# Scatters without mutual waits, a modulation placed behind the routing tables, and 32-token tiles for two more expert places

## The chip, the cores and the metric

The kernel runs on one core of a Trainium2 chip. Its five engines work from queues of their own: TensorE (PE, matrix products), VectorE (DVE), ScalarE (ACT), GpSimd (POOL) and SyncE (SP), the last of which mostly starts transfers. The metric is the device time of one execution in microseconds.

## The reference

The reference computes two layers of a network on 256 tokens (x) and 256 context tokens (ctx) of width 1024, in float32. Layer 0 works on all 512 tokens, layer 1 on the 256 of x. A layer derives six modulation vectors from c by one product, runs a mixer (differential attention beside a convolution of 31 taps, both gated and merged) and then a mixture of 16 experts:

```python
probs = softmax(h @ w_router + b_router)
grouped = probs.reshape(..., N_GROUPS, EXPERTS_PER_GROUP)        # 4 groups of 4
group_sel = argmax(top_k(grouped, 2)[0].sum(-1))                 # one group per token
top_p, top_i = top_k(where(expert_ok, probs, -1.0), 2)           # two experts of that group
for e in range(16):
    y = (silu(h @ w_gate[e]) * (h @ w_up[e])) @ w_down[e]        # 1024 -> 512 -> 1024
    out = out + gates[..., e:e + 1] * y
```

Each part is followed by a residual and a layer norm, with modulation by shift, scale and gate.

## The kernel before

Products that need it are computed in float32 precision from a high and a low part (`whi`, `wlo`): `mm3` issues three matmuls for one. ScalarE writes the high part (`whi<-raw`), VectorE the low part (`wlo<-raw,whi`). The experts with few tokens use plain float32 matmuls, which the profile lists as two entries each (an order of x16 is x32 in the profile).

*Routing.* `route` (lines 914 to 1065) ranks the experts of a layer by their number of tokens and gives each rank one or more places. The last VectorE steps make the tables: `si`, `sf`, `Am`, `Bm`, then eight small matmuls (line 1012), `gidx` (line 1015; which token row stands in which slot) and `sidx` (which result row), then `idx2` and `idx4`, the same for half and quarter rows. GpSimd gathers the token rows of a place by an indirect DMA (`fetch`, line 1156) from `hdr`.

*Modulation.* `ada(l, g, tag)` (from line 366) computes one of three blocks of the modulation vectors with eight loads of `w_ada`, adds the bias (line 382, `modrow`), and for block 0 transposes the result (`tr<-cp,modrow`). Block 0 of layer 1 is computed early, beside the routing of layer 0.

*Places.* `ORDER` (line 141) lists the ranks of a layer in the order of their work. Large ranks use `expert` (128 tokens and more, split products), small ones `expert64` (lines 1277 to 1320) or `expert32` (lines 1327 to 1365). `TINY` (line 107) names the ranks that take `expert32`; `room` gives the tokens that fit (32 or 64). Each is a generator in four steps (gate, up, transposition, down), and the loop in `moe` interleaves the steps of two neighbours: gate n, up n, down n−1. The 1 MB weight halves come through a ring of slots (`raw`, `m0a`, `m0b`, `m1a`), loaded by SyncE in order (line 270), each load as soon as the products on the slot's former contents are done. The down products go to `sc` (line 1310 for 64 tokens, line 1355 for 32), are copied or scaled to `y`, and are scattered to the rows of `ydr` by an indirect DMA of GpSimd (lines 1221, 1267, 1318, 1363). Tokens beyond a place's room go to a list that `overflow` works off in a loop with a count read at run time (`nover`, line 1369), after the last place. Behind it SyncE reads `ydr` back for the sum over the two experts of a token (line 1503). In layer 0 the first two blocks of `w_in` of layer 1 are loaded ahead of that loop (`first_block`).

*Order.* A scheduler places the instructions on each engine, from their dependencies (found by the memory that they touch) and its own estimates. `follow(a, b)` (line 277) keeps a behind b. All scatters of a layer write to the same DRAM array, so each of them counts as dependent on the one before.

Of the kernel before, what the change touches and what calls it, by code (L numbers as in the profile page):

```python
# [103 lines left out]
BIG = ([(2, 2), (3, 1), (4, 1), (5, 1), (6, 1), (7, 1)], [(1, 2), (2, 2), (3, 1)])  # L104
FEW = ([0, 1] + list(range(8, 16)), [0] + list(range(4, 13)))

TINY = (list(range(12, 16)), list(range(6, 13)))
PLACES = (16, 15)


# [50 lines left out]
def dit_kernel(ctx: ExitStack, tc: tile.TileContext, A, out):  # L161
# [205 lines left out]
    def ada(l, g, tag):  # L367

        ps = bank(tag)
        bv = bias.rearrange("(j q) n -> j q n", q=32)  # L370
        src = A["b_ada"][l, g * 2048:(g + 1) * 2048].rearrange("(j n) -> j n", j=4)
        for i in range(2):
            G.dma_start(bv[:, i, :], src)
        for k in range(KC):
            raw = load_raw(A["w_ada"][l, k * 128:(k + 1) * 128, g * 2048:(g + 1) * 2048])
            for j in range(4):
                PE.matmul(ps[32 * j:32 * j + 32, :], cs[:, k, :], raw[:, j * 512:(j + 1) * 512],
                          start=k == 0, stop=k == KC - 1, tile_position=(0, 32 * j))
            if k < KC - 1:
                yield  # L380
        m = small.tile([128, 512], F32, name="modrow", bufs=1)
        V.tensor_tensor(m, ps, bias, op=OP.add)
        if g == 0:
            ps = bank("tr")
            for c in range(4):
                transposed(ps[:, c * 128:(c + 1) * 128], m[:, c * 128:(c + 1) * 128])
            pv = ps.rearrange("p (c j s) -> p c j s", c=4, j=4)
            V.tensor_copy(modT[l][:, :, 0:2, :], pv[:, :, 0:2, 0:2])
            V.tensor_scalar(modT[l][:, :, 2:4, :], pv[:, :, 2:4, 0:2], 1.0, None, op0=OP.add)
        else:  # L390
            dst = moddr[l][:, g * 2048:(g + 1) * 2048].rearrange("s (j n) -> s j n", j=4)
            mv = m.rearrange("(j q) n -> j q n", q=32)
            for i in range(2):
                G.dma_start(dst[i], mv[:, i, :])
        yield
# [518 lines left out]
    def route(l, lg, first):  # L914
# [148 lines left out]
        pool_cm.close()  # L1063
        return erow, sidx, gidx, (idx2, idx4), didx, (cnt, rank, ef)

    def overflow_list(l, pool, cnt, rank, ef, sidx):

        def new(shape, name, dt=F32):
            return pool.tile(shape, dt, name=name)

        def tt_(o, a, b, op):
            V.tensor_tensor(o, a, b, op=op)

        eqc = pool.tile([128, 256], F32, name="v64", bufs=2)[0:1].rearrange("p (a b) -> p a b", a=NE)
        tt_(eqc, rank[0:1, None, :].to_broadcast([1, NE, NE]), C("iota16")[0:1, :, None].to_broadcast([1, NE, NE]),
            OP.is_equal)
        tt_(eqc, eqc, cnt[0:1, None, :].to_broadcast([1, NE, NE]), OP.mult)
        cr = new([1, NE], "cr")
        V.tensor_reduce(cr, eqc, axis=AX.X, op=OP.add)
        no = sum(t[1] for t in OVER[l])  # L1080
        act = new([1, 2, no], "oact")
        eo = new([1, no], "eo", I32)
        so = new([128, no], "so", I32)
        at = 0
        for rk, n, c, least in OVER[l]:
            to, of_ = slice(at, at + n), slice(CAP[l] * rk + c, CAP[l] * (rk + n - 1) + c + 1, CAP[l])
            V.tensor_scalar(act[:, 0, to], cr[:, rk:rk + n], float(least), None, op0=OP.is_gt)
            G.tensor_copy(eo[:, to], ef[:, rk:rk + n])
            G.tensor_copy(so[:, to], sidx[:, of_])
            at += n  # L1090
        tt_(act[:, 1, :], act[:, 0, :], C("iota")[0:1, 1:no + 1], OP.mult)
        nf = new([1, 1], "nf")
        V.tensor_reduce(nf, act[:, 1, :], axis=AX.X, op=OP.max)
        ni = cst.tile([1, 1], I32, name=f"nover{l}")
        V.tensor_copy(ni, nf)
        so_d = dram.tile([128, no], I32, name=f"so_d{l}")
        eo_d = dram.tile([1, no], I32, name=f"eo_d{l}")
        G.dma_start(so_d, so)
        G.dma_start(eo_d, eo)
        return ni, so_d, eo_d  # L1100
# [33 lines left out]
    def moe(l, lg, mh, ml, xn, early, pre_cm, pre):  # L1134
# [64 lines left out]
        def dense(raws, w, xs):  # L1199

            vs, pairs = [], [xs[i:i + 2] for i in range(0, len(xs), 2)]
            for x2 in pairs:
                for ps in up(w, x2, {6: hold["place"]} if x2 is pairs[0] else {}):
                    t = pc.tile([128, DE], F32, name="act", bufs=3)
                    S.activation(t, ps, AF.Tanh, scale=0.5)
                    V.scalar_tensor_tensor(t, t, 1.0, ps, op0=OP.add, op1=OP.mult)
                    vs.append(t)
            hold["split"], hold["logits"] = hold["oh"], None
            w = chunks(raws, 512, ((V, G), (G, V)))
            hold["split"] = None  # L1210
            pu = []
            for i, x2 in enumerate(pairs):
                for v, ps in zip(vs[2 * i:], up(w, x2, {} if i else {1: hold["index"]})):
                    V.scalar_tensor_tensor(v, v, 0.5, ps, op0=OP.mult, op1=OP.mult)
            hold["split"] = hold["gidx"]
            w = chunks(raws, D)
            hold["split"] = None
            ats = [activated(v, True) for v in vs]
            for i, py in enumerate(down(w, ats, "mm")):
                y = outrows(py)  # L1220
                G.indirect_dma_start(out=ydr[l][:, :],
                                     out_offset=bass.IndirectOffsetOnAxis(ap=didx[:, i:i + 1], axis=0),
                                     in_=y, in_offset=None, bounds_check=2 * T - 1, oob_is_err=False)

        def activated(v, rows=False):
            ps = bank("tr")
# [18 lines left out]
        def expert(raws, xs, cols):  # L1245
# [18 lines left out]
            w = chunks(raws, D)  # L1264
            for a, col in zip(ats, cols):
                y = outrows(down(w, [a], "sc")[0])
                G.indirect_dma_start(out=ydr[l][:, :],
                                     out_offset=bass.IndirectOffsetOnAxis(ap=sidx[:, col:col + 1], axis=0),
                                     in_=y, in_offset=None, bounds_check=2 * T - 1, oob_is_err=False)

        def expert64(raws, x, i, whole):

# [42 lines left out]
                V.tensor_tensor(y, py, g2h, op=OP.mult)  # L1315
            else:
                S.copy(y, py)
            G.indirect_dma_start(out=ydr[l].rearrange("t (h d) -> (t h) d", h=2),
                                 out_offset=bass.IndirectOffsetOnAxis(ap=idx2[:, 1, i:i + 1], axis=0),
                                 in_=y, in_offset=None, bounds_check=4 * T - 1, oob_is_err=False)  # L1320

        def expert32(raws, x, i):

# [36 lines left out]
                V.tensor_tensor(y, py[:, :256], g2q, op=OP.mult)  # L1360
            else:
                S.copy(y, py[:, :256])
            G.indirect_dma_start(out=ydr[l].rearrange("t (q d) -> (t q) d", q=4),
                                 out_offset=bass.IndirectOffsetOnAxis(ap=idx4[:, i:i + 1], axis=0),
                                 in_=y, in_offset=None, bounds_check=8 * T - 1, oob_is_err=False)

        def overflow(over, pc):
            ni, so_d, eo_d = over
# [294 lines left out]
```

## Time and profile before

| | us |
|---|---|
| median of 3 runs | 1284.88 (1283.53 to 1286.5) |
| the profiled execution | 1286.37 |
| its span | 1284.4 |
| TensorE busy | 1130.4 (88%) |
| VectorE busy | 748.5 (58%) |
| ScalarE busy | 453.5 (35%) |
| GpSimd busy | 217.9 (17%) |
| mean granted clock | 0.942 |

The span runs from the first to the last instruction of the profiled execution. Layer 0's routing tables end near 458 us, its experts run from 462 to about 730, the layer 1 mixer and routing follow, the small places of layer 1 begin near 1058, its last scatter leaves at 1260, and the rest is the sum over the experts with a layer norm. A row of a timeline is a group of like instructions one after another: start, time from its first start to its last end, engine, line, operation, output and inputs, shape, count; in brackets the idle time of the engine before it and what ended it. "SPq" is SyncE's queue of issued transfers; there the time is that of issuing, with what an issue waited for.

### The profile page before, as it was taken

The numbers are of one execution on the slowest core, as the hardware profiler recorded it, in microseconds if no ns is written. First come the engines' busy times: TensorE is split into PE (matmuls) and PEld (weight loads), VectorE is DVE, ScalarE is ACT, GpSimd is POOL, SyncE is SP. The second block draws the span as 40 slices with busy tenths as digits, with TensorE's granted clock in tenths as the row PEclk, the third lists the DMA queues.
The fourth block names the chain that finished last, engine by engine and source line by source line (L and its number), as shares of the span: only waits on it lengthen the run. The fifth ranks groups of instructions, "written<-read, shape, count | busy, mean of one in ns | idle before, by whom it ended". The sixth has DMA issues, their size and how long they took to land. (4 is left out here: it accounts for less than half of the span.)

```text
span 1284.4 us, 18914 instructions
## 1 busy us (share of the span) xinstructions
PE 1130.4 (88%) x7254; PEld 816.0 (64%) x7254; DVE 748.5 (58%) x1303; ACT 453.5 (35%) x767; POOL 217.9 (17%) x297
## 2 busy tenths in 40 slices
PE   4799999999999869998898558999999799997981
PEld 2476767676878445766666246666888575775751
DVE  0628987766376614355555279996658842424355
ACT  1422223445331504344454233233554621323230
POOL 2500010000000293120100121101100472110111
PEclk9799999997999979999999778999999989998986
DMA  8666651020247979898999698566327579999993
GB/s 307 205 203 224 235 196 66 33 68 32 70 168 287 399 288 394 342 418 344 387 406 417 248 326 296 198 229 225 105 100 284 219 263 372 377 418 426 408 378 110
DMA packets 81452, 336.29 MB, mean 262 GB/s; under 512 B 10398, under 2 KB 10702, under 8 KB 53456
## 3 DMA queue, kind: packets, MB, share of 16 engines
q1 hardware_dynamic: 67072, 303.06, 61.6%
q0 software_dynamic: 10656, 21.11, 4.8%
q10 hardware_dynamic: 3632, 10.90, 2.2%
q8 instruction: 58, 0.95, 0.3%
q14 instruction: 34, 0.28, 0.1%
HBM read 326.16 MB, written 17.57 MB: 268 GB/s over the span
## 5 line engine op out<-in xcount | busy, mean ns | idle before, releaser
L287 DVE TENSOR_TENSOR wlo<-raw,whi 128x1024 fp32r<-128x1024 f32 x196 | 237.9, 1233 | 107.3 <-ACT whi L286 106.2
L286 ACT CAST whi<-raw 128x1024 fp32r<-128x1024 f32 x204 | 209.8, 1049 | 220.2 <-PE mm L321 109.8
L719 DVE SCALAR_TENSOR_TENSOR cv<-cv,cwt,cv 128x512 f32<-128x512 f32 (+1 forms) x240 | 135.4, 611 | 0.7
L317 PE MATMUL mm<-hh,whi 128*128 128x512 f32 (+1 forms) x384 | 131.8, 351 | 2.1 <-ACT hh L513 1.6
L320 PE MATMUL mm<-hl,whi 128*128 128x512 f32 (+1 forms) x384 | 130.1, 343 | 2.7 <-DVE hl L517 2.6
L321 PE MATMUL mm<-hh,wlo 128*128 128x512 f32 (+1 forms) x384 | 129.1, 344 | 0.0
L317 PEld LDWEIGHTS mm<-hh,whi 128*128 128x128 f32 x384 | 73.2, 193 | 21.7 <-issue 8.1
L320 PEld LDWEIGHTS mm<-hl,whi 128*128 128x128 f32 x384 | 73.5, 192 | 16.7 <-issue 6.1
L321 PEld LDWEIGHTS mm<-hh,wlo 128*128 128x128 f32 x384 | 72.8, 192 | 14.9 <-issue 7.2
L320 PE MATMUL mm<-wlo,xt 128*128 128x512 f32 x192 | 78.1, 408 | 0.4
L317 PE MATMUL mm<-whi,xt 128*128 128x512 f32 x192 | 75.8, 403 | 1.7 <-ACT whi L286 1.7
L321 PE MATMUL mm<-whi,xt 128*128 128x512 f32 x192 | 76.8, 401 | 0.0
L320 PE MATMUL mm<-wlo,hh 128*128 128x512 f32 x176 | 70.4, 400 | 1.4 <-DVE wlo L287 1.4
L317 PE MATMUL mm<-whi,hh 128*128 128x512 f32 x176 | 69.7, 403 | 0.0
L321 PE MATMUL mm<-whi,hl 128*128 128x512 f32 x176 | 69.5, 396 | 0.0
L320 PEld LDWEIGHTS mm<-wlo,xt 128*128 128x128 f32 x192 | 37.0, 193 | 13.7 <-DVE wlo L287 4.0
L1289 PE MATMUL mm<-raw,xt 128*64 128x256 f32 x384 | 45.2, 382 | 0.0
L320 PE MATMUL sc<-wlo,at 128*128 128x512 f32 x96 | 41.1, 428 | 3.3 <-DVE wlo L287 3.1
L317 PEld LDWEIGHTS mm<-whi,xt 128*128 128x128 f32 x192 | 36.8, 193 | 10.9 <-ACT whi L286 2.6
L317 PEld LDWEIGHTS mm<-whi,hh 128*128 128x128 f32 x176 | 33.4, 190 | 15.8 <-issue 5.9
L321 PEld LDWEIGHTS mm<-whi,xt 128*128 128x128 f32 x192 | 37.0, 193 | 7.1
L668 DVE TENSOR_REDUCE mx<-sc 128x1 f32<-128x512 f32 (+1 forms) x48 | 28.4, 599 | 22.1 <-PE sc L663 21.9
(407 smaller groups left out, 2175.8 us busy)
## 6 DMA issues: line engine op xcount, KB each, us to landing
raw<-in_w_ada_dram SPq DMA_DIRECT2D x48, 1024.0 KB
raw<-in_w_e_down_dram SPq DMA_DIRECT2D x47, 1024.0 KB
raw<-in_w_e_up_dram SPq DMA_DIRECT2D x44, 1024.0 KB
raw<-in_w_e_gate_dram SPq DMA_DIRECT2D x41, 1024.0 KB
raw<-in_w_in_dram SPq DMA_DIRECT2D x36, 1024.0 KB
m0a<-in_w_e_up_dram SPq DMA_DIRECT2D x10, 1024.0 KB
raw<-in_w_out_dram SPq DMA_DIRECT2D x8, 1024.0 KB
m0b<-in_w_e_gate_dram SPq DMA_DIRECT2D x8, 1024.0 KB
```

The lines of the kernel that those rows point to most:

```text
L286: j = S.copy(hi, src)
L287: i = eng.tensor_tensor(lo, src, hi.bitcast(F32), op=OP.subtract)
L317: i = PE.matmul(ps, lhs[0], rhs[0], start=first, stop=False)
L320: PE.matmul(ps, lhs[0], rhs[1], start=False, stop=False)
L321: PE.matmul(ps, lhs[1], rhs[0], start=False, stop=last)
L668: V.tensor_reduce(mx[:, m:m + 1], pS[:, :n], axis=AX.X, op=OP.max, negate=True)
L719: i = V.scalar_tensor_tensor(av, win, cwt[:, cb, j:j + 1], av, op0=OP.mult, op1=OP.add)
L1289: PE.matmul(ps[64 * j:64 * j + 64, u * 256:u * 256 + 256], xt[:, k, k0 // 4, :], raw[:, k * 512 + j * 256:k * 512 + j * 256 + 256], start= ...
```

## The change

The scatters of a layer are declared independent of one another, by a helper that replaces the four direct calls of `dense`, `expert`, `expert64` and `expert32`. The reason given is that no two places hold the same row. The scatter inside the overflow loop stays as it was. The add of `modrow` for block 0 of layer 1 has to come behind the table `idx2`. `TINY[1]` starts at rank 4 rather than rank 6, so that places 4 and 5 of layer 1 (ranks by number of tokens) use `expert32`, gather 64 half rows rather than 128, and have room for 32 tokens; the overflow list of layer 1 is made from three entries rather than four.

```diff
-TINY = (list(range(12, 16)), list(range(6, 13)))
+TINY = (list(range(12, 16)), list(range(4, 13)))
...
         m = small.tile([128, 512], F32, name="modrow", bufs=1)
-        V.tensor_tensor(m, ps, bias, op=OP.add)
+        i = V.tensor_tensor(m, ps, bias, op=OP.add)
+        if l and g == 0:
+            follow(i, hold["route"])
...
+    def scatter(l, view, **kw):
+
+        i = G.indirect_dma_start(out=view, in_offset=None, oob_is_err=False, **kw)
+        for other in scattered[l]:
+            tc.declare_no_dep(i.ins, other.ins, reason="no two slots hold the same row")
+        scattered[l].append(i)
+
+    scattered = ([], [])
...
-            G.indirect_dma_start(out=ydr[l].rearrange("t (h d) -> (t h) d", h=2),
-                                 out_offset=bass.IndirectOffsetOnAxis(ap=idx2[:, 1, i:i + 1], axis=0),
-                                 in_=y, in_offset=None, bounds_check=4 * T - 1, oob_is_err=False)
+            scatter(l, ydr[l].rearrange("t (h d) -> (t h) d", h=2),
+                    out_offset=bass.IndirectOffsetOnAxis(ap=idx2[:, 1, i:i + 1], axis=0), in_=y, bounds_check=4 * T - 1)
```

The three other sites are replaced in the same way. Since the dependencies differ, the scheduler draws up another order. Three places follow. Line numbers of the new kernel are up to 9 higher. SyncE loads the weights in practically the same order as before.

The first is VectorE at the routing tables of layer 0. Before:

```order
L1002 TENSOR_SCALAR si<-si 128x8
L382 TENSOR_TENSOR modrow<-mm,bias 128x512
L1004 CAST sf<-si 128x16
L1007 TENSOR_TENSOR Am<-cp,sf 128x512
L1011 TENSOR_SCALAR Bm<-cp,sf 128x128 x4
L388 COPY modT_104<-tr 128x4x4
L389 TENSOR_SCALAR modT_104<-tr 128x4x4
L1011 TENSOR_SCALAR Bm<-cp,sf 128x128 x3
L1622 TENSOR_TENSOR gt_5826<-modT_104,pt_598 128x8
L1011 TENSOR_SCALAR Bm<-cp,sf 128x128
L1623 TENSOR_TENSOR bt_5827<-modT_104,pt_598 128x8
L1622 TENSOR_TENSOR gt_5826<-modT_104,pt_598 128x8
```

Now:

```order
L1004 TENSOR_SCALAR si<-si 128x8
L1006 CAST sf<-si 128x16
L1009 TENSOR_TENSOR Am<-cp,sf 128x512
L1013 TENSOR_SCALAR Bm<-cp,sf 128x128 x8
L1017 TENSOR_SCALAR gidx<-sc 128x64
L1019 TENSOR_SCALAR sidx<-sc 128x64
L1023 TENSOR_TENSOR cmp<-rank,cp 1x256
L930 TENSOR_TENSOR cmp<-cmp,cp 1x256
L1029 TENSOR_REDUCE ef<-cmp 1x16
L1031 CAST erow<-ef 1x16
L1055 TENSOR_SCALAR idx_3323<-four,cp 128x4
L1053 TENSOR_SCALAR idx_3321<-both,cp 128x20
```

Before, `modrow` stood between `si` and `sf`, and its transposed copies (`modT`, `gt`, `bt`) between the pieces of `Bm`; `gidx` came three rows below the last one shown. Now the tables come first, and `modrow` follows directly behind the last row shown.

The second is TensorE at the end of layer 0's experts. `sc<-raw_5562` and `sc<-raw_5568` are the down products of the last place but one (rank 11, 64 tokens), `xt_5517` are the tokens of the last place (rank 15), `v_5615` its hidden values, and `nover` the count of the overflow loop. Before:

```order
L321 MATMUL sc<-whi,at 128x512
L1335 MATMUL mm<-raw,xt_5517 32x128 x16
L1335 MATMUL mm<-m0a,xt_5517 32x128 x16
L324 MATMUL tr<-cp,v_5615 128x128
L1310 MATMUL sc<-raw_5562,at_5559 64x512 x4
L1310 MATMUL sc<-raw_5568,at_5559 64x512 x4
L1355 MATMUL sc<-raw,at_5621 32x256 x16
L1369 TENSOR_LOAD nover_5704
```

Now:

```order
L1343 MATMUL mm<-raw_5520,xt_5517 32x128 x9
L1343 MATMUL mm<-raw_5538,xt_5517 32x128 x16
L1319 MATMUL sc<-raw_5562,at_5559 64x512 x4
L1319 MATMUL sc<-raw_5568,at_5559 64x512 x4
L1343 MATMUL mm<-raw,xt_5517 32x128 x16
L1343 MATMUL mm<-m0a,xt_5517 32x128 x16
L324 MATMUL tr<-cp,v_5615 128x128
L1363 MATMUL sc<-raw,at_5621 32x256 x16
L1376 TENSOR_LOAD nover_5704
```

The down products of rank 11 have moved from behind the transposition of the last place to ahead of its up products. At five more places of layer 0 the down products of a place moved in the same way, ahead of the end of the next place's up products.

The third is TensorE at the end of layer 1's experts, where `sc<-whi` and `sc<-wlo` are the split down products of rank 3, `mm<-raw_10628` (now `raw_10706`) the last up products of the last place, and `sc<-raw_10655` and `sc<-m0a` (now `raw_10733`) its down products. Before:

```order
L321 MATMUL sc<-whi,at 128x512
L317 MATMUL sc<-whi,at 128x512
L320 MATMUL sc<-wlo,at 128x512
L321 MATMUL sc<-whi,at 128x512
L1335 MATMUL mm<-raw_10628,xt_10511 32x128 x16
L324 MATMUL tr<-cp,v_10646 128x128
L1355 MATMUL sc<-raw_10655,at_10652 32x256 x8
L1355 MATMUL sc<-m0a,at_10652 32x256 x8
L1369 TENSOR_LOAD nover_10712
```

Now:

```order
L321 MATMUL sc<-whi,at 128x512
L317 MATMUL sc<-whi,at 128x512 x2
L1343 MATMUL mm<-raw_10688,xt_10589 32x128 x7
L320 MATMUL sc<-wlo,at 128x512
L321 MATMUL sc<-whi,at 128x512
L320 MATMUL sc<-wlo,at 128x512
L321 MATMUL sc<-whi,at 128x512
L1343 MATMUL mm<-raw_10688,xt_10589 32x128 x9
L1343 MATMUL mm<-raw_10706,xt_10589 32x128 x16
L324 MATMUL tr<-cp,v_10724 128x128
L1363 MATMUL sc<-raw_10733,at_10730 32x256 x8
L1363 MATMUL sc<-m0a,at_10730 32x256 x8
```

Before, all split products of rank 3 stood ahead of the last up products; now a part of these stands between the split products. The down products of the place before the last (`sc<-m0a,at_10423`, now `at_10501`) were scattered in pieces of one to eight among the up products of rank 3; now they stand in two blocks of eight.

## Rows read from the trace of the kernel before

**Rows 1.** Timeline of VectorE, 445 to 450: start us, us, engine, line, operation [idle <-releaser].

```profile
445.84 0.69 DVE L382 TENSOR_TENSOR modrow<-mm,bias 128x512 f32<-128x512 f32 x1 [2.66 <-PE mm L377]
...
449.96 0.23 DVE L1015 TENSOR_SCALAR gidx<-sc 128x64 int32<-128x64 f32 x1
```

**Rows 2.** Timeline of TensorE, 444 to 458.

```profile
444.71 1.07 PE L377 MATMUL mm<-raw,cs 128*32 128x512 f32 x8 [0.33 <-DMA raw<-in_w_ada_dram]
...
447.66 0.97 PE L1012 MATMUL sc<-Am,Bm 128*128 128x64 f16 x4 [0.41 <-DVE Bm L1011]
...
457.67 1.19 PE L324 MATMUL tr<-cp,xg 64*128 64x64 f32 x8 [7.74 <-DMA xg<-hdr,gidx]
```

**Rows 3.** Timeline of GpSimd, first gather.

```profile
451.04 1.02 POOL L1156 DMA_INDIRECT xg<-hdr,gidx  x1 [3.01 <-DVE bt L1624]
```

**Rows 4.** Waits of TensorE, 480 to 715: total us, times, longest us.

```profile
PE tr L324 <- DVE v L1297: 3.8, 3, 1.5
PE tr L324 <- DVE act L1260: 3.1, 4, 0.8
```

**Rows 5.** Timeline of TensorE, end of layer 0's experts.

```profile
713.28 1.12 PE L1335 MATMUL mm<-raw,xt 128*32 128x128 f32 x32 [1.17 <-DMA raw<-in_w_e_up_dram]
...
720.20 6.54 PE L1310 MATMUL sc<-raw,at 128*64 128x512 f32 x16 [0.84 <-ACT y L1196]
726.67 1.93 PE L1355 MATMUL sc<-raw,at 128*32 128x256 f32 x32
```

**Rows 6.** Timeline of GpSimd, same stretch.

```profile
727.69 0.98 POOL L1318 DMA_INDIRECT ydr<-y,idx  x1 [5.80 <-ACT y L1317]
732.86 0.98 POOL L1363 DMA_INDIRECT ydr<-y,idx  x1 [4.19 <-DMA ydr<-y,idx]
```

**Rows 7.** Timeline of SyncE's queue, same stretch.

```profile
703.51 2.60 SPq L270 DMA_DIRECT2D raw<-in_w_e_down_dram  x2
714.46 12.62 SPq L270 DMA_DIRECT2D raw<-in_w_in_dram  x2
735.96 1.28 SPq L1503 DMA_DIRECT2D ah<-ydr  x2
```

**Rows 8.** Timeline of ScalarE, same stretch.

```profile
729.12 0.37 ACT L1362 COPY y<-sc 128x256 f32<-128x256 f32 x1 [1.70 <-PE sc L1355]
731.87 1.99 ACT L286 CAST whi<-raw 128x1024 fp32r<-128x1024 f32 x2 [2.38 <-SPq L1370]
```

**Rows 9.** Windows: us, busy us (x instructions) of each engine, PEclk, DMA share, GB/s.

```profile
750.00:800.00 50.00, 40.77 (x281) 33.26 (x278) 45.26 (x95) 19.30 (x32) 11.78 (x21) 0.86 0.88 313
1115.00:1120.00 5.00, 5.00 (x72) 2.48 (x76) 2.09 (x3) 0.34 (x1) 0.45 (x1) 1.00 0.61 211
1120.00:1125.00 5.00, 5.00 (x98) 4.22 (x87) 3.46 (x7) 2.39 (x5) 1.29 (x1) 1.00 0.92 333
...
1245.00:1250.00 5.00, 5.00 (x85) 3.84 (x85) 3.56 (x4) 1.65 (x2) 0.85 (x1) 1.00 0.89 374
1250.00:1255.00 5.00, 5.00 (x47) 3.98 (x49) 1.30 (x3) 0.00 (x0) 0.00 (x0) 1.00 0.06 21
```

**Rows 10.** Waits of SyncE's queue, 1066 to 1122, columns as in rows 4.

```profile
SPq L270 <- PE sc L1310: 17.9, 6, 10.3
```

**Rows 11.** Timeline of TensorE, 64-token places of layer 1.

```profile
1077.84 3.62 PE L1289 MATMUL mm<-raw,xt 128*64 128x256 f32 x32
...
1114.88 3.65 PE L1310 MATMUL sc<-raw,at 128*64 128x512 f32 x16
```

**Rows 12.** Timeline of TensorE, end of layer 1's experts.

```profile
1234.87 0.63 PE L1355 MATMUL sc<-m0a,at 128*32 128x256 f32 x4
1235.42 0.50 PE L320 MATMUL mm<-wlo,xt 128*128 128x512 f32 x1
...
1258.20 1.05 PE L1355 MATMUL sc<-m0a,at 128*32 128x256 f32 x16
```

**Rows 13.** Timeline of GpSimd, last scatter.

```profile
1260.01 0.98 POOL L1363 DMA_INDIRECT ydr<-y,idx  x1 [3.69 <-DVEq L1370]
```

More of the change, by code (lines that the diff above doesn't have):

```diff
@@ L1220, in dense @@
                 y = outrows(py)
-                G.indirect_dma_start(out=ydr[l][:, :],
-                                     out_offset=bass.IndirectOffsetOnAxis(ap=didx[:, i:i + 1], axis=0),
-                                     in_=y, in_offset=None, bounds_check=2 * T - 1, oob_is_err=False)
+                scatter(l, ydr[l][:, :], out_offset=bass.IndirectOffsetOnAxis(ap=didx[:, i:i + 1], axis=0),
+                        in_=y, bounds_check=2 * T - 1)
         def activated(v, rows=False):
@@ L1266, in expert @@
                 y = outrows(down(w, [a], "sc")[0])
-                G.indirect_dma_start(out=ydr[l][:, :],
-                                     out_offset=bass.IndirectOffsetOnAxis(ap=sidx[:, col:col + 1], axis=0),
-                                     in_=y, in_offset=None, bounds_check=2 * T - 1, oob_is_err=False)
+                scatter(l, ydr[l][:, :], out_offset=bass.IndirectOffsetOnAxis(ap=sidx[:, col:col + 1], axis=0),
+                        in_=y, bounds_check=2 * T - 1)
         def expert64(raws, x, i, whole):
@@ L1362, in expert32 @@
                 S.copy(y, py[:, :256])
-            G.indirect_dma_start(out=ydr[l].rearrange("t (q d) -> (t q) d", q=4),
-                                 out_offset=bass.IndirectOffsetOnAxis(ap=idx4[:, i:i + 1], axis=0),
-                                 in_=y, in_offset=None, bounds_check=8 * T - 1, oob_is_err=False)
+            scatter(l, ydr[l].rearrange("t (q d) -> (t q) d", q=4),
+                    out_offset=bass.IndirectOffsetOnAxis(ap=idx4[:, i:i + 1], axis=0), in_=y, bounds_check=8 * T - 1)
         def overflow(over, pc):
```

## The prediction

> **What bounds the kernel now.** I read the stages one after another, because one average over the run says little here. First the timeline around the routing tables of layer 0, where three engines hand one result on. VectorE stands still for 2.66 us in front of `modrow`, for modulation products that TensorE ends at 444.71 + 1.07 = 445.78, and only behind it come the routing casts, the index matmuls, `gidx` and the first gather [rows 1 to 3]. The experts of layer 0 cannot start before that gather. Then the waits of TensorE in 480 to 715: the longest are short ones on VectorE (3.8 us in 3 and 3.1 us in 4), so TensorE sets the pace there [rows 4]. Then the turn from layer 0 to layer 1: TensorE does the down products of the last two experts (6.54 us, then 1.93 us), a scatter waits 4.19 us for the scatter ahead of it, and the reads of `ydr` leave at 735.96 [rows 5 to 7]. In layer 1 I read the windows: the queues are full except for a hole, with a DMA share of 0.61 and 0.92 in 1115 to 1125 where a busy stretch has 1.00; SyncE waited up to 10.3 us there for down products of a 64-token place to free a slot [rows 9, 10]. At the end the transfers stop near 1249.5 (share 0.89, then 0.06), but TensorE still has work until 1259, and the last scatter leaves at 1260.01 [rows 9, 12, 13].
>
> **The change part by part.** The profiled execution took 1286.37 us (span 1284.4), 1.5 above the median of 1284.88. The terms are differences inside that execution and I take them off the median.
>
> *The early modulation behind the tables.* VectorE's wait (2.66) and the add behind it (0.69) leave the path to `gidx`: 3.3 us. TensorE cannot begin the index matmuls before 445.78, but then `Bm` is ready; from their first to `gidx` it took 449.96 − 447.66 = 2.3 us, with waits on `Bm` between, so `gidx` comes between 446.7 and 448.1 instead of at 449.96 [rows 1, 2]. The gather of 451.04 moves along, since POOL waited 3.01 us in front of it [rows 3]; the two bias transfers go behind the tables there, and their result is wanted a whole layer later. The four transposes of `modrow` now stand ahead of the first `xg` transposes, which waited 7.74 us for the gather [rows 2], and that hides them. If the gather itself is held by the store of `hdr`, nothing is won. I take **−3.3** (0 to −3.6), since the add, too, goes from VectorE's queue ahead of the tables.
>
> *Scatters without waits, inside layer 0.* No wait of TensorE there names a scatter, but the order of TensorE is drawn up anew: at six places the down products of an expert go in ahead of the transposes of the next, that is into the waits of 3.8 and 3.1 us [rows 4]. That can give up to −6.9. Against it, the number of changes between products that use 128, 64 and 32 columns of the array rises from 72 to 86 in these experts. What one costs shows where four entries of 32-column products stand between 128-column ones: 1235.42 − 1234.87 = 0.55 us, against 4 × 1.93/32 = 0.24, so 0.31 for two changes, 0.16 each [rows 5, 12]. Fourteen more make +2.2. The two sides are near each other in size and I put **0** (−6.9 to +2.2). The Trainium skill ("TensorEngine Tiling (Array Packing)", Key Properties) says that a change of the tiling mode, not of the tile alone, drains TensorE; this speaks against such mixing, and the row agrees, with 0.16 us as its price.
>
> *The turn to layer 1.* Before, the down products of the place ahead of the last stand at 720.20, behind everything; now they stand ahead of the last up products, where TensorE waited 1.17 us at 713.28 [rows 5]. They take 3.65 us at a fast stretch (the same shape at 1114.88 [rows 11]), so the last up products and the transposition come up to a microsecond later, and the last down products start near 720.5 instead of 726.67. From their start to the scatter it took 729.5 − 726.67 without the wait, so the scatter leaves near 723 instead of 732.86. From that to the reads it took 735.96 − 732.86 = 3.1 [rows 6 to 8]; beside a busy queue the scatter before needed 732.86 − 727.69 = 5.2. So by this chain the reads leave at 726 to 728. What is late next is the second block of `w_in`: its load waited for a slot until about 727 (714.46 + 12.62), its casts ran from 731.87 [rows 7, 8]. Its slot now comes free with the last expert's first down weights near 721.2; 4.8 us of transfer as before and 2 us of casts end at 728.3. I take that: 728.3 − 735.96 = **−7.7** (−3 if the load still waits, −9 if the casts slip behind the reads).
>
> *Two more places with 32-token tiles.* The gate and up products of a 64-token place are two such groups as at 1077.84 (2 × 3.62), its down products one of 3.65: 10.9 us. Those of a 32-token place are four such groups as at 713.28 (4 × 1.12) and one of 1.93: 6.4 us [rows 5, 11]. That is 4.5 each, 9 us of TensorE for both, and half of the gathers' rows. But from 1070 to 1115 the transfers are saturated, so TensorE's time is not the run's. What it gives is slots freed before the queue runs dry, so the hole: (0.39 + 0.08) × 5 = **−2.3** (0 to −2.4) [rows 9].
>
> *The end of layer 1.* In the new order the down products of the second last expert are one block ahead of the transposes of the dense part, and the last up products are mixed into the split down products, so the tail of 128-column products no longer stands between the last load and the end. From the last landing (1249.5) to the scatter it was 1260.01 − 1249.5 = 10.5 us. The chain that must remain behind the last load is one set of products (1.05), y and the issue, some 2 to 3 us [rows 9, 12, 13]. That would be −8. Since TensorE worked through from 1250 to 1255 and not all of that can have gone ahead of the last weights, I take **−7** (0 to −9).
>
> *Redrawn order elsewhere.* The mixer of layer 1 has other positions on VectorE and TensorE, without one direction. TensorE is idle there for 50 − 40.77 = 9.2 us of 50 [rows 9]; its ends are −9.2 and +9.2. Since the change gives no reason for a gain, I charge a quarter, **+2.3**.
>
> Sum: −3.3 + 0 − 7.7 − 2.3 − 7 + 2.3 = −18.0, from 1284.9: **1267 us**. Taking the ranges together the likeliest case lies in 1259 to 1274.
>
> **The rivals.** (1) *One of the two ends gives nothing.* For: each rests on one order, and the wait that goes may be replaced by a later one (the block of `w_in`; the last weights). Against: the rows show TensorE and not the transfers as late in both. It costs 7.7 or 7, so about 1274. (2) *Both ends stay*, as a slot or a load holds them: −3.3 − 2.3 + 2.3 leaves −3.3, with the 2.2 for the changes of shape −1.1: 1281.6 to 1284. (3) *Slower: the down products moved ahead stall TensorE.* TensorE works in order, so at the six places of layer 0 everything behind waits when the down weights have not landed. One expert's are two loads of 1 MB, 5.0 us at the 420 GB/s of a full queue (374 at a share of 0.89 [rows 9]); when both are missing at all six that is +30, so about 1297. It decides from 18/6 = 3.0 us a place. For: SyncE loads in an unchanged order, and it put the down loads of 703.51 only 10 us ahead of their new use [rows 7]. Against: TensorE's waits there show no large one on DMA, and what is loaded behind them waits too. (4) *The change doesn't do what it says*: a token count over 32 at place 4 or 5 would send the overflow loop round, with 6 MB of weights (some 15 us at 420 GB/s) for each, and end near 1282. The counts of layer 1 in the reference's inputs at these places are 8 and 4.
>
> **How the numbers follow.** Forecast 0.58, one end only 0.22, both stay 0.08, stalled down products 0.10, overflow 0.02. A measurement here tells 0.2%, about 2.6 us, from no change: faster is below 1282.3, slower above 1287.5. Forecast and one end are faster (0.80), of the case in which both stay a quarter is (0.02), so 0.82; the rest of it, 0.06, and the overflow give 0.08 for the same; the stalled products are slower, 0.10. The range is 1258 to 1284: it leaves out the slower case and a tenth of the forecast's, which leaves 0.8 inside.
>
> **What would show it.** In the profile after: no VectorE wait before the casts of the routing and the first gather near 448; scatters that never wait for `ydr`; the reads of layer 0's result some 11 us earlier in the run, of which 3 come from the start; a DMA share near 1.0 through the hole; the last scatter 2 to 4 us behind the last landing. I am wrong if TensorE shows long waits on `raw<-in_w_e_down` in layer 0, if the second `w_in` block still sets the turn, or if the mixer of layer 1 is longer by more than 5 us.

## The result and the profile after

The changed kernel took 1265.18 us (median of 4 runs, 1264.60 to 1266.33) against 1284.2 for the kernel before beside it: a ratio of 0.9859, with a 95% interval of 0.9827 to 0.9891. A second set of runs on another occasion gave 0.9881 (0.9852 to 0.9909). The forecast was 1267. Its sum came out within 2 us, but not its terms. Two executions among the experiments below (2773.17 us of "modulation alone", 5498.52 us of "last but one held") are left out of the ratios. The table shows where the time went, by marks that both kernels have. Two profiled executions of each kernel are shown, as a measure of how far one and the same program differs. "MB" are the bytes that the transfers have moved since the last integer step of `si` on VectorE, added up from windows of 2 us.

| stretch (us) | forecast | before, twice | changed, twice | difference of the means |
|---|---|---|---|---|
| last step of `si` to 14 MB | −3.3 | 44.5, 44.8 | 41.3, 42.0 | −3.0 |
| 14 MB to 94 MB (experts of layer 0) | 0 | 207.1, 206.8 | 196.9, 199.8 | −8.6 |
| 94 MB to the reads of `ydr` (the turn) | −7.7 | 41.3, 41.6 | 40.2, 41.0 | −0.8 |
| these reads to layer 1's first gather | +2.3 | 297.1, 298.9 | 295.0, 295.2 | −2.9 |
| that to the last scatter of layer 1 | −9.3 | 226.9, 222.9 | 222.3, 221.5 | −3.0 |
| last scatter to the end | 0 | 24.4, 25.3 | 24.1, 24.6 | −0.5 |
| sum | −18.0 | | | −18.8 |

Two executions are few. In four of the executions below TensorE does layer 0's experts in the order of the kernel before (before, before again, modulation alone, 32-token tiles alone), and in six in that of the changed kernel (changed, changed again, scatters alone, changed with small buffers, the end of layer 1 in another order, the index matmuls first). From 14 MB to 94 MB the four took 203.4 to 207.1 us (205.4 on average) and the six 196.9 to 202.0 (199.5). So the new order is worth some 6 us there, not 8.6. The mixer took 297.6 us on average in the same four and 295.8 in nine with the new order, so some 2 us, not 2.9.

**The tables of layer 0.** VectorE after the change (start us, us, engine, line, operation, in brackets idle time and releaser):

```profile
443.20 0.17 DVE L1006 CAST sf<-si 128x16 f32<-128x16 int32 x1
...
446.27 1.11 DVE L1013 TENSOR_SCALAR Bm<-cp,sf 128x128 f16<-128x128 f32 x4 [1.13 <-PE sc L1014]
447.68 0.23 DVE L1017 TENSOR_SCALAR gidx<-sc 128x64 int32<-128x64 f32 x1 [0.30 <-PE sc L1014]
...
455.37 0.68 DVE L382 TENSOR_TENSOR modrow<-mm,bias 128x512 f32<-128x512 f32 x1
```

TensorE in the same stretch:

```profile
445.03 1.07 PE L377 MATMUL mm<-raw,cs 128*32 128x512 f32 x8 [1.74 <-DMA raw<-in_w_ada_dram]
...
446.67 0.97 PE L1014 MATMUL sc<-Am,Bm 128*128 128x64 f16 x4 [0.35 <-DVE Bm L1013]
```

The casts follow each other, `modrow` has gone behind the table, and `gidx` starts at 447.68, 2.3 us earlier [rows 1], and the first gather at 448.75 instead of 451.04 [rows 3]. A new, shorter wait has come up: the second four `Bm` wait 1.13 us for the index matmuls, which wait until TensorE is through with the modulation products at 446.10 [rows 2].

**The experts of layer 0.** Windows of the kernel before in which transfers had holes (columns as in rows 9; the last three are PEclk, DMA share, GB/s):

```profile
520.00:530.00 10.00, 10.00 (x102) 6.29 (x102) 3.64 (x4) 2.58 (x3) 1.01 (x1) 1.00 0.54 205
590.00:600.00 10.00, 8.30 (x107) 5.03 (x109) 2.67 (x4) 2.64 (x5) 0.00 (x0) 1.00 0.65 244
630.00:640.00 10.00, 8.41 (x79) 4.96 (x75) 3.70 (x5) 4.38 (x7) 0.00 (x0) 1.00 0.77 307
```

The same windows of the changed kernel:

```profile
520.00:530.00 10.00, 10.00 (x160) 7.29 (x157) 6.22 (x8) 4.37 (x7) 1.01 (x1) 1.00 0.90 333
590.00:600.00 10.00, 7.62 (x142) 6.13 (x135) 5.40 (x8) 5.43 (x9) 1.48 (x2) 1.00 1.00 409
630.00:640.00 10.00, 9.68 (x35) 7.42 (x36) 8.76 (x8) 8.64 (x11) 0.98 (x1) 0.83 1.02 419
```

Waits of SyncE's queue from 480 to 700, before (us in total, times, longest):

```profile
SPq L270 <- PE sc L1310: 38.4, 10, 10.6
...
SPq L270 <- PE sc L1355: 15.8, 4, 11.8
```

And changed, where lines 1319 and 1363 are the same products:

```profile
SPq L270 <- PE sc L1319: 24.3, 8, 10.6
...
SPq L270 <- PE sc L1363: 5.1, 4, 1.8
```

Before, loads waited 54.2 us for down products of small places to give back their weight slots; now 29.4 us. The three holes were worth 10 × (0.46 + 0.35 + 0.23) = 10.4 us of transfer, and about one is left. The waits do not measure the holes, though. The longest wait for a 64-token place, 10.6 us, lies directly at the first hole in both kernels (it ends at 525.9 before, at 520.6 now), and two kernels below keep 55.9 and 46.7 us of such waits.

**The turn to layer 1.** TensorE, GpSimd, ScalarE and SyncE at the end of layer 0, changed:

```profile
704.03 3.65 PE L1319 MATMUL sc<-raw,at 128*64 128x512 f32 x16
707.61 1.12 PE L1343 MATMUL mm<-raw,xt 128*32 128x128 f32 x32
...
711.33 0.33 PE L324 MATMUL tr<-cp,v 128*128 128x128 f32 x1 [1.69 <-DVE v L1351]
712.01 3.47 PE L1363 MATMUL sc<-raw,at 128*32 128x256 f32 x32 [0.35 <-ACT at L1356]
```

```profile
708.63 0.98 POOL L1070 DMA_INDIRECT ydr<-y,idx  x1 [4.35 <-ACT y L1326]
716.22 0.98 POOL L1070 DMA_INDIRECT ydr<-y,idx  x1 [6.61 <-ACT y L1370]
721.48 1.05 POOL L586 MEMSET cv<- 128x1144 f32 x1 [4.28 <-ACTq L1377]
```

```profile
719.21 1.99 ACT L286 CAST whi<-raw 128x1024 fp32r<-128x1024 f32 x2 [1.37 <-SPq L1377]
```

```profile
709.18 5.02 SPq L270 DMA_DIRECT2D raw<-in_w_in_dram  x2
721.44 1.36 SPq L1510 DMA_DIRECT2D ah<-ydr  x2
```

The down products of the last place but one (704.03) stand ahead of the last up products, as the new order says, and no engine waits for a scatter [rows 5, 6]. Against the 94 MB the last scatter comes 3 us sooner (35.0 and 35.9 us behind them; before, 38.2 and 38.4). But it no longer holds the reads. Between the places and the reads stands the overflow loop (line 1377). There GpSimd waits 4.28 us for ScalarE's queue, and ahead of the loop ScalarE has the casts of the second `w_in` block, which end at 721.20, 0.24 us ahead of the reads. In all nine executions with independent scatters these casts end 0.23 to 0.25 us ahead of the reads, while the last scatter stands 4.8 to 6.1 us ahead of them. In the four with the order of the kernel before it is the other way round: the scatter stands 3.1 us ahead in each, the casts end 2.0 to 2.1 us ahead [rows 6 to 8]. So the second `w_in` block sets the turn now. Its load waits for the slot of the last down products and is issued 32.6 and 33.5 us behind the 94 MB, no sooner than before (32.1 and 31.5). These products took 3.47 us at a granted clock of 0.53, where they took 1.93 us at 1.00 before [rows 5].

**The end of layer 1.** Windows of the changed kernel:

```profile
1175.00:1180.00 5.00, 5.00 (x103) 3.64 (x101) 1.79 (x3) 0.00 (x0) 0.98 (x1) 1.00 0.86 323
1225.00:1230.00 5.00, 5.00 (x35) 3.51 (x34) 3.12 (x5) 1.15 (x2) 0.00 (x0) 1.00 1.01 418
1230.00:1235.00 5.00, 2.72 (x60) 2.02 (x63) 2.92 (x14) 0.54 (x2) 0.97 (x1) 0.95 0.41 163
1235.00:1240.00 5.00, 2.99 (x29) 1.09 (x20) 0.42 (x1) 0.00 (x0) 0.98 (x1) 0.71 0.01 3
```

TensorE and the last scatter there:

```profile
1222.73 0.73 PE L317 MATMUL sc<-whi,at 128*128 128x512 f32 x2 [0.81 <-ACT whi L286]
...
1229.99 1.79 PE L1343 MATMUL mm<-raw,xt 128*32 128x128 f32 x50
1233.70 0.33 PE L324 MATMUL tr<-cp,v 128*128 128x128 f32 x1 [1.92 <-DVE v L1351]
1234.38 1.90 PE L1363 MATMUL sc<-raw,at 128*32 128x256 f32 x16 [0.36 <-ACT at L1356]
1236.04 1.95 PE L1363 MATMUL sc<-m0a,at 128*32 128x256 f32 x16
```

```profile
1238.74 0.98 POOL L1070 DMA_INDIRECT ydr<-y,idx  x1 [6.57 <-DVEq L1377]
```

Where before a hole of 0.39 and one of 0.08 stood [rows 9], 82 us behind the first gather, the transfers are now full; a new hole of 0.14 stands at 1175, 159 us behind it. The transfers end near 1232, and the last scatter leaves 6.7 us later; before that was 10.5. Behind the last split products come the last place's up products (until 1231.8), the activation (1.92 us of TensorE idle), the transposition, and two sets of down products of 1.90 and 1.95 us. Before, these took 1.07 and 1.05 at a granted clock of 1.00 [rows 12]; here the granted clock over them was 0.53. That is not the new order's doing alone: in four more executions with the same idle time (the changed kernel with small buffers, the two with held products, the index matmuls first) it stayed at 1.00, and they took 1.07 and 1.05.

### The profile page after: what moved, and what is told of

The parts are those of the page before. It is cut to its first block, busy times and chain, and to the rows that moved or that the text cites. A ratio compares the mean times of both kernels' runs of the same rounds, so it can differ in the third digit from the quotient of the medians.

```text
span 1262.8 us, 19232 instructions
## 1 busy us (share of the span) xinstructions
PE 1110.4 (88%) x7412; PEld 809.5 (64%) x7412; DVE 747.4 (59%) x1302; ACT 451.9 (36%) x767; POOL 217.3 (17%) x295
## 5 line engine op out<-in xcount | busy, mean ns | idle before, releaser
L287 DVE TENSOR_TENSOR wlo<-raw,whi 128x1024 fp32r<-128x1024 f32 x196 | 237.4, 1232 | 95.5 <-ACT whi L286 91.9
L1070 POOL DMA_INDIRECT ydr<-y,idx x20 | 20.6, 1029 | 186.5 <-DVE y L1368 96.4
L320 PE MATMUL sc<-wlo,at 128*128 128x512 f32 x96 | 40.2, 419 | 2.7 <-DVE wlo L287 2.6
```

Of the source, the lines that this page charges most:

```text
L287: i = eng.tensor_tensor(lo, src, hi.bitcast(F32), op=OP.subtract)
L320: PE.matmul(ps, lhs[0], rhs[1], start=False, stop=False)
L1070: i = G.indirect_dma_start(out=view, in_offset=None, oob_is_err=False, **kw)
```

## The experiments

The columns of the table are as above; "20 to 30" and "40 to 60" are the times in which the transfers came from 20 to 30 MB, and from 40 to 60. The two lie where the holes at 520 and 590 were. One execution each.

| kernel | ratio to before (95% interval) | 14 MB | 20 to 30 | 40 to 60 | 94 MB | reads | mixer | layer 1 |
|---|---|---|---|---|---|---|---|---|
| before | | 44.5 | 29.5 | 53.0 | 251.6 | 292.9 | 297.1 | 226.9 |
| before again | 1.0016 (0.9996 to 1.0037) | 44.8 | 29.9 | 52.6 | 251.6 | 293.2 | 298.9 | 222.9 |
| changed | 0.9859 (0.9827 to 0.9891) | 41.3 | 26.0 | 48.2 | 238.2 | 278.4 | 295.0 | 222.3 |
| changed again | 0.9881 (0.9852 to 0.9909) | 42.0 | 26.4 | 49.0 | 241.8 | 282.8 | 295.2 | 221.5 |
| scatters alone | 0.9911 (0.9890 to 0.9932) | 45.1 | 27.4 | 47.6 | 242.6 | 282.7 | 295.1 | 222.3 |
| modulation alone | 0.9975 (0.9956 to 0.9993) | 41.1 | 27.1 | 51.6 | 244.6 | 286.1 | 297.3 | 224.3 |
| 32-token tiles alone | 1.0002 (0.9981 to 1.0024) | 44.1 | 27.1 | 50.8 | 248.2 | 290.6 | 297.0 | 223.8 |
| before, small buffers | 0.9899 (0.9882 to 0.9916) | 44.4 | 27.8 | 49.3 | 246.1 | 285.8 | 294.7 | 224.5 |
| four places held | 0.9909 (0.9881 to 0.9938) | 41.7 | 29.4 | 47.8 | 243.1 | 282.2 | 295.9 | 220.6 |
| last but one held | 0.9844 (0.9818 to 0.9870) | 41.8 | 26.8 | 49.0 | 244.2 | 283.9 | 294.4 | 220.5 |
| changed, small buffers | 0.9885 (0.9859 to 0.9911) | 41.8 | 26.1 | 49.3 | 241.8 | 281.8 | 295.5 | 221.8 |
| end of layer 1 in another order | 0.9869 (0.9841 to 0.9897) | 41.9 | 28.5 | 48.6 | 243.9 | 285.5 | 296.4 | 221.8 |
| three edits together | 0.9852 (0.9823 to 0.9881) | 40.7 | 29.1 | 48.6 | 241.0 | 279.5 | 297.9 | 221.3 |
| index matmuls first | one run | 42.5 | 29.6 | 48.4 | 243.3 | 283.4 | 296.7 | 220.4 |

**Scatters alone.** The changed kernel without its two other edits:

```diff
-TINY = (list(range(12, 16)), list(range(4, 13)))
+TINY = (list(range(12, 16)), list(range(6, 13)))
...
-        if l and g == 0:
-            follow(i, hold["route"])
```

> Only the scatters made independent in both layers; the early modulation and the 32-token places stay as before. Theory (the independent scatters let down products move ahead, which frees weight slots sooner and fills holes in layer 0's transfers): about 12 us of the shift at layer 0's end, some 2 more in the mixer behind it and 3 at layer 1's end, so 1266 to 1270; reads of ydr in layer 0 near 724, DMA share at 590 to 600 and 630 to 640 near 1.0. Rival (the parts need each other, and the 32-token places carry the end of layer 1): 1275 or more, with the last scatter of layer 1 no closer to the last load than before (10.5 us).

Measured 1269.28, a ratio of 0.9911: some 11 us, of 15 to 18 for the whole change. The stages say the same: 9 us by 94 MB, 2 in the mixer. The windows at 590 and 630 are full (1.02 and 1.01). The theory's figures hold, except that layer 1 shows no clear 3 us, since before itself gave 226.9 and 222.9 there.

**Modulation alone.**

```diff
-        V.tensor_tensor(m, ps, bias, op=OP.add)
+        i = V.tensor_tensor(m, ps, bias, op=OP.add)
+        if l and g == 0:
+            follow(i, hold["route"])
```

> Only the early modulation placed behind the routing tables. Theory: the first gather comes 2.3 us sooner, all of layer 0's experts with it, and the end by the same, 1282. Rival (layer 0's experts are limited by transfers that don't start sooner): the gather comes sooner but the last scatter of layer 0 does not, 1284.

Measured 1277.47 against 1281.4, a ratio of 0.9975: −3.2 us, with −0.9 to −5.6 in the interval. The 14 MB come 3.5 us sooner, and this lasts to the end of layer 0. (The profiled execution was the fastest of all, 1273.83 us, so its later stages overstate it.) The rival is out.

**32-token tiles alone.**

```diff
-TINY = (list(range(12, 16)), list(range(6, 13)))
+TINY = (list(range(12, 16)), list(range(4, 13)))
```

> Only the 32-token tiles at places 4 and 5 of layer 1. Theory: the hole in layer 1's transfers near 1115 to 1125 closes, 2 to 3 us, 1282; the rest of the end stays at 10 us behind the last load. Rival 1: transfers are saturated over the whole of layer 1 and move the hole elsewhere, 1284. Rival 2: TensorE's 9 us come off the end, 1276.

Measured a ratio of 1.0002 (0.9981 to 1.0024): nothing that shows. In layer 1 the first 40 MB are in 108.1 us behind the first gather, against 111.3 and 110.1 before, so the hole does close; at 75 MB it is 193.3 against 195.4 and 194.0, so a part of the lead is lost again by the end. A hole with a share of 0.87 opens 160 us behind the first gather, where the kernel before had 0.99 and 0.91; the changed kernel has one there too (0.86 at 1175). Rival 1 is nearest.

**Small buffers, before.** Scatters depend on one another as before:

```diff
-            y = pc.tile([128, D], F32, name="y", bufs=2)[:, :256]
+            y = pc.tile([128, 256], F32, name="y32", bufs=2)
```

> The kernel before, with the scatters still dependent on one another, but the 32-token places write their results to two small buffers of their own in place of the two shared ones. Theory (the wait between scatters is what holds down products back): little, within 3 us of before. Rival (it is the two shared result buffers, which come free only when a scatter has landed, that hold the down products back): the down products move ahead here too and most of the gain of the independent scatters comes, 1270 to 1276.

Measured 1270.12, a ratio of 0.9899: as much as the independent scatters (0.9911), and my theory fell. The scatters still wait in this run, as GpSimd shows at the end of layer 0:

```profile
716.47 0.98 POOL L1318 DMA_INDIRECT ydr<-y,idx  x1 [8.15 <-DMA ydr<-y,sidx]
722.41 1.71 POOL L1363 DMA_INDIRECT ydr<-y,idx  x1 [4.96 <-DVE wlo L287]
```

8.15 us of waiting for the scatter ahead, twice what the kernel before showed [rows 6], and the kernel is 12.9 us faster all the same. What the two edits have in common is a new order: in both, the scheduler puts the down products of layer 0's last place but one ahead of the last up products, and draws the mixer anew (294.7 here, 295.0 with the change). The orders are not the same, though: of the six places of layer 0 whose down products move ahead with the change, three (those of 64 tokens) do so here, and the loads still wait 55.9 us for down products. So the wait between scatters is not what cost the time; which part of the order did is open.

**The changed kernel again**, unchanged.

> The changed kernel once more, on the same chip as the three that follow, as their yardstick: 1262 to 1267, with the four parts between the routing's last cast and the end (tables, experts of layer 0 with the turn, mixer of layer 1, experts of layer 1) within 3 us of its first profile.

1267.51, half a microsecond above the range; only layer 0 differed by more than the 3 us expected (282.8 to the reads against 278.4).

**Four places held.** The down step loads its weights as before, but its products are put behind the next gate products:

```diff
+            two = [next(raws) for _ in range(2)]
+            if l == 0:
+                yield
             py = bank("sc")
...
+                        if held and k0 + k + j == 0:
+                            follow(m, held.pop())
...
+            held[:] = [hold["gate"]] if l == 0 and isinstance(task, int) else []
+            next(late, None)
```

> The changed kernel, scatters independent, but in layer 0 the down products of the four places whose next neighbour is a large expert are held behind the gate products of the place after that, about where they stood before. Theory (the gain of layer 0 comes from down products that stand earlier and free their weight slots earlier): holes in layer 0's transfers come back, and 4 to 9 us of the gain are lost, 1269 to 1274. Rival (it comes from scatters that don't wait in the run): as the changed kernel, 1265.

Measured 1269.83 (six runs, 1265.25 to 1274.57), a ratio of 0.9909; with 0.9881 for the changed kernel beside it the intervals overlap, so the time does not decide. The windows:

```profile
520.00:530.00 10.00, 10.00 (x106) 6.57 (x103) 5.28 (x8) 3.73 (x6) 1.01 (x1) 1.00 0.67 232
590.00:600.00 10.00, 9.73 (x101) 7.24 (x98) 7.33 (x9) 8.65 (x13) 2.96 (x2) 1.00 1.01 416
630.00:640.00 10.00, 10.00 (x41) 8.11 (x41) 8.44 (x8) 7.65 (x10) 0.98 (x1) 0.90 1.01 420
```

The hole at 520 seems back (0.67; 0.90 in the changed kernel), and 20 to 30 MB take 29.4 us, as before. But the change never touched TensorE's order around that hole, and with the changed kernel's order of layer 0 the same window had a share from 0.58 (index matmuls first, 29.6 us) and 0.74 (end of layer 1 in another order) to 0.99 (changed, small buffers). So the first hole differs from execution to execution and shows nothing here. The hole at 590 is not back (1.01), and 40 to 60 MB take 47.8, although the loads wait 46.7 us for down products again (29.4 in the changed kernel). So this run speaks against the theory that the earlier down products close the holes by freeing slots. That 40 to 60 MB pass sooner holds in every execution with the scatters independent (47.6 to 49.3 us, against 50.8 to 53.0 in the four with the order of before); what carries it is not settled.

**Last but one held.** The down step is split as in the run before, and the last place but one is held:

```diff
+            held[:] = [hold["gate"]] if l == 0 and n == len(order) - 1 else []
             next(before, None)
```

> The changed kernel, but in layer 0 the down products of the last place but one are held behind the last place's up products, as before. Theory (the turn to layer 1 waits for TensorE's last products): the last scatter of layer 0 comes 2 to 4 us later against the first up products' weights, and so does the end, 1268. Rival (the second block of w_in or the landing of the last scatter sets the turn anyhow): less than 1.5 us, 1265.

Measured 1263.64, a ratio of 0.9844: no loss at all. From 94 MB to the reads it took 39.7 us, against 40.2 and 41.0. The second `w_in` block sets the reads here too (its casts end 0.23 us ahead of them), as the rival has it. But the run changes one thing more: the held products fill the time in which TensorE stood idle, and the last down products are fast again.

```profile
718.38 1.93 PE L1371 MATMUL sc<-raw,at 128*32 128x256 f32 x32 [0.64 <-ACT at L1361]
```

The 1.5 us that this gives back (3.47 in the changed kernel) go against what the later place costs; the two were not separated.

**Small buffers, changed kernel**, with the diff of the small buffers above.

> The changed kernel with two small result buffers of their own for the 32-token places. Theory (with independent scatters the shared buffers come free in time): no change, within 2 us of the changed kernel. Rival (the buffers still hold places back): 3 to 5 us faster, 1261.

Measured 1266.59 against 1267.51: the same. Either of the two edits gives the gain, and both together give no more.

**The end of layer 1 in another order.**

```diff
-            if n == len(order) - 1:
+            if n == len(order) - 1 and not last:
                 next(before, None)
```

> The changed kernel, but at the end of layer 1 the up products of the last place (and their weights) come ahead of the split down products of rank 3. Theory (behind the last load stand the last place's up products, its activation and transposition, not only its down products): the last scatter comes 3 us closer to the last landing, from 8 us to 5, and the end comes 3 us sooner, 1263. Rival (the split products of rank 3, now later, take their place): no change or 1 to 3 us slower, 1266 to 1269.

Measured 1270.24, a ratio of 0.9869 (0.9841 to 0.9897): no gain. From the first gather to the last scatter it took 221.8 us, as in the changed kernel (222.3, 221.5). TensorE there:

```profile
1229.97 1.12 PE L1343 MATMUL mm<-raw,xt 128*32 128x128 f32 x32 [0.85 <-DMA raw<-in_w_e_up_dram]
1232.41 0.30 PE L324 MATMUL tr<-cp,v 128*128 128x128 f32 x1 [1.33 <-DVE v L1351]
1233.74 1.18 PE L317 MATMUL sc<-whi,at 128*128 128x512 f32 x2 [1.02 <-ACT whi L286]
...
1241.65 1.07 PE L1363 MATMUL sc<-raw,at 128*32 128x256 f32 x16 [0.33 <-DVE y L1205]
1242.54 1.05 PE L1363 MATMUL sc<-m0a,at 128*32 128x256 f32 x16
```

The last place's up products are done at 1231.1, early as planned, but now the split products of rank 3 wait for their casts and run until 1241.3, directly ahead of the last down products. The rival is right.

**Three edits together**: the end of layer 1 as above, the last but one held, and the next edit.

> The changed kernel with three edits: the order of the end of layer 1 as in the run before this one, the down products of layer 0's last place but one behind the last place's up products, and the last modulation products behind the index matmuls. Theory: 3 us from the end, 1 from the tables, nothing from the other, 1262. Rival (nothing adds up, since transfers set both layers): 1265.

Measured 1265.31, a ratio of 0.9852 (0.9823 to 0.9881): the same as the changed kernel. No version beat it clearly.

**The index matmuls first.**

```diff
-                PE.matmul(ps[32 * j:32 * j + 32, :], cs[:, k, :], raw[:, j * 512:(j + 1) * 512],
+                i = PE.matmul(ps[32 * j:32 * j + 32, :], cs[:, k, :], raw[:, j * 512:(j + 1) * 512],
...
+                if l and g == 0 and k == KC - 1 and j == 0:
+                    follow(i, hold["index"])
```

> The changed kernel with the last four modulation products behind the eight index matmuls, so that TensorE is free for these when their inputs are there. Theory (behind the removed wait of VectorE it was TensorE, at work on the modulation, that set the tables): from the last cast of si to gidx 3.6 to 4.0 us, where the changed kernel has 4.7 to 5.0. Rival (VectorE's own row of pieces of Bm sets it): 4.7.

VectorE and TensorE there:

```profile
444.29 0.17 DVE L1008 CAST sf<-si 128x16 f32<-128x16 int32 x1
...
445.11 2.25 DVE L1015 TENSOR_SCALAR Bm<-cp,sf 128x128 f16<-128x128 f32 x8
447.66 0.23 DVE L1019 TENSOR_SCALAR gidx<-sc 128x64 int32<-128x64 f32 x1 [0.30 <-PE sc L1016]
```

```profile
446.65 0.97 PE L1016 MATMUL sc<-Am,Bm 128*128 128x64 f16 x4 [0.17 <-DVE Bm L1015]
447.55 1.06 PE L377 MATMUL mm<-raw,cs 128*32 128x512 f32 x8
```

From the last step of `si` (444.09) to `gidx` it took 3.57 us, where the changed kernel took 4.67 and 4.95: the wait inside `Bm` is gone, as the theory has it. One execution took 1270.91, so no gain in time was seen.

**The kernel before again.**

> The kernel before once more, unchanged, as a measure of how far its stages differ from one execution to another. Theory (the stages of the first profile are typical within 3 us): from the last cast of si to the reads of layer 0's result 288 to 294 us, from these to layer 1's first gather 297, from that to the last scatter 224 to 227; the ratio to itself 1 within 0.3%. Rival (the first profile was an outlier in layer 0): below 287 for the first of these.

A ratio of 1.0016 to itself. Layer 0 came out as in the first profile, layer 1 4 us shorter (222.9 against 226.9, expected 224 to 227). So the difference of 3.0 us in layer 1 is no larger than what one program shows between two executions.

## Why the prediction was right, and where it was not

*The tables*: right in mechanism and nearly in size. `gidx` gained 2.0 to 2.3 us, not 3.3, because TensorE's modulation products set it next. The working had named that bound (446.7 to 448.1; it came at 447.68), and then took the full wait of VectorE all the same. The 14 MB came 3.0 us sooner.

*The scatters inside layer 0, "I put 0 (−6.9 to +2.2)"*: this is the step that failed most. It took TensorE to set the pace there, priced the new order by the waits of TensorE [rows 4] alone, and set a charge for changes of shape against them. The stage came 8.6 us shorter in the first executions, and some 6 over all with these orders. The holes in the transfers stood in another view, 10.4 us in the profiled execution. I had used that argument for layer 1 (slots freed before the queue runs dry) and not here, where the holes were larger. Its holes come nearer to the size, but the experiments do not show its mechanism: two kernels whose loads still wait 55.9 and 46.7 us for down products took 201.7 and 201.4 us for the stage, inside the range of the new order (196.9 to 202.0). The gain comes with the new order; what in it closes the holes stays open. The charge for 14 more changes of shape was not tested by itself; the stage as a whole shows no loss. The rival of stalled down products is out: in the changed kernel TensorE shows no wait for a down weight in layer 0 up to 712.

*The turn, −7.7*: it failed, −0.8 measured. The prediction let the slot of the second `w_in` block come free some 6 us sooner, by last down products that start sooner. It came free no sooner against the loads (32.6 and 33.5 us behind the 94 MB, before 32.1 and 31.5). The last scatter gained 3 us where some 10 were forecast, and its gain is lost behind it, since the casts of that block hold the reads. The term also took 1.93 us for the last down products, which took 3.47 at the lower clock. (Its own parts, 721.2 + 4.8 + 2, give 728.0 and not 728.3.) By its own test the prediction said it was wrong "if the second `w_in` block still sets the turn", and the block does, though the working itself had put it next.

*The 32-token tiles, −2.3*: the hole closed, but alone it is worth nothing that shows (1.0002), since another opens later. *The end of layer 1, −7*: mis-sized. The term counted one set of products, `y` and the issue behind the last load, 2 to 3 us; it was 6.7, since the last up products, the activation, the transposition and two sets of down products came behind it too, these in the profiled execution at a lower clock. The two together gave −3.0 instead of −9.3.

*The mixer, +2.3*: wrong in sign, −2.9 in the first executions and some −2 over all. The kernel with small buffers draws yet another order there and gains the same (294.7); why these orders are better was not tested.

So 17 us forecast for the turn, the tiles and layer 1's end came as 4, and 8.6 (or 6) unforeseen came from layer 0's experts: errors of both signs that cancelled. That the sum met the forecast is luck. Of the three edits the scatters gave about 11 us, the modulation 3, the tiles none alone; the sum of 14.3 lies within the interval of the whole (14.0 to 22.2 below 1284.2 by the first ratio).

## What to carry to other kernels

Where transfers are nearly full, look at the holes in the transfers before pricing an earlier product by the idle time of the engine that does it. What the load queue waits for says where to look, but it is no price: here kernels with 29.4, 46.7 and 55.9 us of such waits took about the same time. A false dependence can cost through the order that a scheduler draws from it and not through its wait: before taking it away, look whether a buffer or another edit draws as good an order. And profile the kernel before twice, or use the stages that an experiment leaves alone: a stage of 220 us differed by 4 us between two executions of one program, and a hole by a share of 0.58 to 0.99 with one order of TensorE, as much as several of the terms.

## What was not expected of the hardware

The granted clock fell behind short idle times, but not each time. At the turn, TensorE stood idle for 1.7 us and, behind one transposition, 0.35 more; in all seven executions of this kind the last down products then took 3.07 to 3.62 us (granted clock 0.53 to 0.61), and 1.93 us at 1.00 where the idle time was filled. At the end of layer 1, behind 1.92 us of idle time and 0.36 more, two sets took 1.90 and 1.95 us (granted clock 0.53). Of the seven executions of this kind three showed such a fall, and four, with 1.95 to 1.97 us of idle time, kept 1.00 and took 1.07 and 1.05 us.
